# An encoder kernel: early small inputs, other banks for a second block, the router's comparisons first, a small expert last

## The chip, the cores and the metric

The kernel runs as one program on one core of a Trainium2 chip. The metric is device time in microseconds (us) for one execution, lower is better. Engines are TensorE (PE; PEld are its weight loads), VectorE (DVE), ScalarE (ACT), GpSimd (POOL) and SyncE (SP), which issues most of the transfers. Each runs its own list of instructions in order and waits for the others by semaphores.

## What is computed

A hybrid encoder of two layers on 256 tokens of width 1024, in float32. Cut to what matters here:

```python
def reference(x, positions, norm_mix, w_in_first, ..., norm_out):
    for l in range(DEPTH):                       # 2
        h = rmsnorm(x, norm_mix[l])
        proj = h @ (w_in_first if l == 0 else w_in_rest[l - 1])
        # columns of proj: RWKV-7 heads, differential attention, mean pooling
        x = x + jnp.concatenate([y_a, y_b, y_c], axis=-1) @ w_out[l]
        h = rmsnorm(x, norm_ffn[l])
        if l % 2 == 0:
            x = x + swiglu(h, ffn_gate[i], ffn_up[i], ffn_down[i])
        else:
            x = x + moe_swiglu(h, router[i], exp_gate[i], exp_up[i], exp_down[i])
    return rmsnorm(x, norm_out)

def moe_swiglu(h, router, w_gate, w_up, w_down):
    logits = t @ router
    top_val, top_idx = lax.top_k(logits, TOP_K)  # 2 of 8 experts
    gates = jax.nn.softmax(top_val, axis=-1)
    combine = jnp.sum(jax.nn.one_hot(top_idx, N_EXPERTS) * gates[..., None], axis=1)
    for e in range(N_EXPERTS):
        out = out + combine[:, e:e + 1] * swiglu(t, w_gate[e], w_up[e], w_down[e])
```

D_FF is 3584. Each expert has three matrices of 1024 x 3584.

## The kernel before, in words

Weights come in tiles of 128 x 1024 float32 (512 KB) through a ring of raw slots (`wload`). Most are split in two halves of a reduced format that TensorE takes in one pass: ACT casts the tile to the high half (L201, `whi`), VectorE subtracts that from the tile (L209, `wlo`; a few go to POOL), and the product is three matmuls (`mm3`): high x high, low x high, high x low. The loads are issued by SP in the order of their use (L198, L184); a load waits for its slot, a cast for its load and a free high slot.

**The start** (layer 0's mixer, 0 to some 195 us). `setup_x` loads the identity, the rows of small vectors and x on SP and transposes x on TensorE (L230). Then two weight loads follow, and six more in the k loop over the 1024 rows of `w_in_first`: eight steps of 8 blocks x 3 matmuls into four banks (L226). The constants (`consts`, `consts2`), `lambda_q`, `lambda_k` and `positions` are loaded on ACT's queue (L311, L313, L341, L353) behind ACT's work on the norm. VectorE's use of them (`rksel` L327, `lamq` L342, `posf` L355, `ang` L358) stands between its weight splits. After the k loop VectorE makes `u` from the sums (L551) and `us` from it (L548, L549), and goes on to the pooling sums `cs` and to splits of later weights.

**The dense layer** (some 195 to 435 us). 3584 columns go in seven blocks of 512. `gateup(c0)` makes gate and up sums of one block in four banks of the pool `pa`; VectorE scales them to `gu` (L1307). `down(c0 - 1)` runs after `gateup(c0)` and adds into four banks of `pr`. So each block's `gateup` takes the four `pa` banks again that the block before has used.

**The router** (some 616 us). TensorE makes the logits, VectorE copies them (`lg`, L1018), compares them pairwise (`cmp`, L1444 to L1447; the last of these multiplies by constants), sums the comparisons to ranks and makes the selection `sel` (L1449). TensorE counts it with a triangle of ones (`tri`), VectorE makes places `pos` (L1461) and the one-hot gather matrix `Pm` (L1555), and TensorE gathers the tokens of an expert. At the same time x is split in two halves, the high one on ACT (L1424), the low one on POOL (L1425, twice 128 x 1024), and the first expert weights are split; `EPOOL` names the tiles whose low half POOL makes. `keep_clock` issues matmuls whose result nobody reads.

**The experts** (some 616 to 1519 us). Experts 0 and 1 keep their places, the other six are put in places 2 to 7 by their counts of tokens, the three with the fewest in the places 2, 4 and 6. Those three are "few": at most 64 tokens, run with plain float32 weights, without splits. A step of a full expert is a block of 512 columns: 8 tiles for gate and up and 4 for down, 72 three-pass matmuls; seven steps are 84 tiles. A few expert has the same 84 tiles with fewer matmuls. `SEQ` is the order of the places. `down` of a step runs after the `gateup` of the next one; `silu` (L1651), `turn` and the sums of `combine` (L1743, L1754) or `combine_few` (L1685, L1694) are woven into the step behind. After the last step come the last `combine`, the norm and the output (`final`, L1841 to L1853). `issue_after` sets the place of an instruction in its own engine's list; it adds no wait between engines.

The order on VectorE, ACT, POOL and SP is set by a scheduler from these hints; TensorE's is the order in which the code is written.

Of the kernel before, what the change touches and what calls it, by code (L numbers as in the profile page):

```python
# [7 lines left out]
F32 = mybir.dt.float32  # L8
# [75 lines left out]
SEQ = (0, 2, 1, 3, 4, 5, 6, 7)  # L84
# [15 lines left out]
GC0 = 2  # L100
WARM = (7, 5)
# [5 lines left out]
class K:  # L107
# [172 lines left out]
    def setup_x(self, P):  # L280
# [18 lines left out]
    def setup(self, P):  # L299
        nc, A, cp, mc, v, dv = self.nc, self.A, self.cp, self.mc, self.v, self.dv  # L300
# [6 lines left out]
        self.rks, tmp = mc.tile([128, 4, 2], F32, name="rksel"), self.dtmp  # L307
# [3 lines left out]
        nc.scalar.dma_start(c, A["consts"][:, :C_W])  # L311
        self.c2 = cp.tile([128, C_ALL - C_IOTA], F32, name="consts2")
        nc.scalar.dma_start(self.c2, A["consts"][:, C_IOTA:])  # L313
# [20 lines left out]
    def setup2(self, sp):  # L334
        nc, A, cp, c = self.nc, self.A, self.mc, self.c
        q = nc.scalar

        lq = sp.tile([128, 256], F32, name="lamq", tag="s1k", bufs=2)
        lk = sp.tile([128, 256], F32, name="lamk", tag="s1k", bufs=2)
        for t_, nm in ((lq, "lambda_q"), (lk, "lambda_k")):  # L340
            q.dma_start(t_, bass.AP(tensor=A[nm].tensor, offset=A[nm].offset, ap=[[0, 128], [1, 256]]))  # L341
# [136 lines left out]
    def mixer(self, l, P):  # L478
# [801 lines left out]
    def ffn(self, l, P):  # L1280
# [9 lines left out]
        def gateup(c0):  # L1290
            bs = [self.bank() for _ in range(4)]
# [24 lines left out]
        def down(c0, ah, al, last=False):  # L1316
            if not acc:
                acc.extend(self.bank("pr") for _ in range(4))
# [8 lines left out]
            if not last:  # L1327
                for f in range(4):
                    w = ld(f)
                    for a in range(2):  # L1330
# [4 lines left out]
                          lambda a: self.norm_part((a,), (("pa",) * 4, ("pr", "pr", "pa", "pa"))[a]),  # L1335
# [12 lines left out]
    def moe(self, l, P):  # L1348
# [71 lines left out]

        x0 = [[P.tile([128, D], F32R, name=f"x{n}{a}", tag=("xp r0", "r1 r2")[a].split()[n]) for a in range(2)] for n in range(2)]
        for a in range(2):
            with self.tc.issue_after(self.hi) if a else nullcontext():
                nc.scalar.copy(x0[0][a], self.x[:, a])  # L1424
            nc.gpsimd.tensor_sub(x0[1][a], self.x[:, a], x0[0][a].bitcast(F32))  # L1425
        parts = [[[t_[:, k2 * 256:k2 * 256 + 256] for t_ in x0[n]] for n in range(2)] for k2 in range(4)]
        self.hi_after = self.hi
        ahead, self.ahead = self.ahead, []
        for n_ in range(len(ahead), XSPLIT + 3):
            self.early = [nc.gpsimd if n_ in EPOOL else nc.vector]  # L1430
            self.lo_after = self.pow if n_ > 3 else None
            ahead.append(wgu(0, 0, n_ // 2, n_ % 2))
            if n_ == 3:
                with self.tc.issue_after(self.w1):
                    for a in range(2):
                        self.stat(a, P.tile([128, D], F32, name="nsq", tag="gh0"))
# [481 lines left out]
```

## Time and profile before

| | us |
|---|---|
| median of three runs | 1536.27 (1534.88, 1536.27, 1536.39) |
| profiled execution | 1537.17 |
| its span, first to last instruction | 1535.4 |
| TensorE busy | 1454.0 (95%) |
| VectorE, ACT, POOL busy | 996.8, 812.5, 163.7 |
| HBM read | 431.75 MB, 282 GB/s over the span |
| mean granted clock | 0.982 |

Busy shares are means over stages with different limits. The chain is followed backwards from the last instruction to what released each step. In a timeline row the bracket holds the idle time of the engine just before and what ended it. "SPq" and "ACTq" are the issuing of transfers. [...]

### The profile page before, as it was taken

How to read it: one execution, taken by the hardware profiler on the slowest of the kernel's cores; microseconds unless marked ns; L12 is line 12 of the kernel's file. 1: busy time of each engine (PE TensorE's matmuls, PEld its weight loads, DVE VectorE, ACT ScalarE, POOL GpSimd, SP SyncE). 2: the span in 40 equal slices, each digit the busy share in tenths (PEclk: the TensorE clock that was granted, in tenths of full speed). 3: DMA queues.
4: the chain of work that ended last, by engine and by line, in shares of the span. 5: the costliest groups of instructions: out<-in, count | busy, mean ns of one | idle time of the engine just before them, and what ended most of it. 6: DMA issues, size and time to landing. Idle time of an engine off the chain costs nothing.

```text
span 1535.4 us, 27152 instructions
## 1 busy us (share of the span) xinstructions
PE 1454.0 (95%) x10215; PEld 1102.3 (72%) x10215; DVE 996.8 (65%) x1318; ACT 812.5 (53%) x1146; POOL 163.7 (11%) x153
## 2 busy tenths in 40 slices
PE   6889989999998999899998999999998999998996
PEld 6767789999987777688633688888534787435885
DVE  4875665556659755899511889898412897206896
ACT  4635454444445454688501778777302775205785
POOL 2442100000025323300000000011000000000001
PEclk9999999999999999999999999999999999999999
DMA  7322346666543238689799999999999999999991
GB/s 228 110 72 98 110 167 190 192 187 189 162 119 98 86 111 326 213 306 368 281 419 412 412 410 412 410 382 336 374 418 412 412 410 402 405 416 411 411 411 38
DMA packets 172457, 434.67 MB, mean 283 GB/s; under 512 B 14834, under 2 KB 18013, under 8 KB 172317
## 3 DMA queue, kind: packets, MB, share of 16 engines
q1 hardware_dynamic: 170924, 430.74, 75.5%
q8 instruction: 82, 1.34, 0.3%
q10 hardware_dynamic: 848, 0.99, 0.3%
q0 software_dynamic: 544, 1.12, 0.3%
q14 instruction: 59, 0.48, 0.1%
HBM read 431.75 MB, written 1.05 MB: 282 GB/s over the span
## 4 chain that ended last, share of the span: by engine, by line
PE 73%; DVE 10%; DMA 9%; ACT 4%; issue 3%; POOL 1%; ACTq 0%; SPq 0%; DVEq 0%; POOLq 0%
PE ps L226 71%; DMA r<-in_exp_up 5%; PE ps L230 3%; DMA r<-in_exp_gate 2%; DVE wlo L209 2%; DVE wlox L209 1%; DMA lamk<-in_lambda_k 1%; ACT whi L201 1%; DMA raw<-in_w_in_rest 1%; DVE us L549 0%; ACT whix L201 0%; DVE us L548 0%; ACT nsq L389 0%; DMA x<-in_x 0%; ACT hT_h L409 0%
## 5 line engine op out<-in xcount | busy, mean ns | idle before, releaser
L209 DVE TENSOR_TENSOR wlo<-r,whi 128x1024 fp32r<-128x1024 f32 x193 | 233.5, 1237 | 43.8 <-ACT whi L201 42.4
L201 ACT CAST whi<-r 128x1024 fp32r<-128x1024 f32 x196 | 202.7, 1055 | 37.2 <-DMA r<-in_exp_gate 17.4
L209 DVE TENSOR_TENSOR wlox<-r,whix 128x1024 fp32r<-128x1024 f32 x125 | 152.2, 1238 | 63.8 <-ACT whix L201 58.0
L201 ACT CAST whi<-raw 128x1024 fp32r<-128x1024 f32 x117 | 123.1, 1054 | 95.9 <-PE ps L226 86.0
L209 DVE TENSOR_TENSOR wlo<-raw,whi 128x1024 fp32r<-128x1024 f32 x106 | 133.9, 1267 | 55.0 <-ACT whi L201 54.5
L201 ACT CAST whix<-r 128x1024 fp32r<-128x1024 f32 x125 | 130.2, 1055 | 39.2 <-DMA r<-in_exp_gate 26.8
L226 PE MATMUL ps<-whi,gf 128*128 128x512 f32 x396 | 134.6, 398 | 0.0
L226 PE MATMUL ps<-r,gs 128*64 128x512 f32 (+1 forms) x636 | 131.1, 549 | 1.9 <-DMA r<-in_exp_up 1.9
L226 PE MATMUL ps<-fT,whi 128*128 128x256 f32 x544 | 99.3, 285 | 3.8 <-DVE gu L1307 3.4
L226 PE MATMUL ps<-whix,gf 128*128 128x512 f32 x276 | 95.4, 400 | 2.5 <-ACT whix L201 2.5
L226 PEld LDWEIGHTS ps<-r,gs 128*64 128x64 f32 x636 | 42.5, 136 | 72.6 <-issue 60.6
L1418 POOL TENSOR_TENSOR xp<-x,xp 128x512 fp32r<-128x512 f32 x12 | 22.6, 1886 | 628.9 <-ACT xp L1417 583.4
L226 PEld LDWEIGHTS ps<-fT,whi 128*128 128x128 f32 x544 | 85.0, 192 | 5.2 <-issue 4.0
L226 PEld LDWEIGHTS ps<-whi,gf 128*128 128x128 f32 x396 | 75.3, 190 | 18.6 <-issue 1.6
L1664 ACT COPY mah<-ps 128x512 f32<-128x512 f32 (+1 forms) x12 | 6.4, 532 | 142.2 <-PE ps L230 142.2
L226 PE MATMUL ps<-wlo,gf 128*128 128x512 f32 x198 | 78.5, 396 | 0.3
L226 PE MATMUL ps<-fT,wlo 128*128 128x256 f32 x272 | 77.2, 284 | 0.0
L209 DVE TENSOR_TENSOR wlox<-raw,whix 128x1024 fp32r<-128x1024 f32 x49 | 61.2, 1251 | 17.7 <-ACT whix L201 17.6
L226 PE MATMUL ps<-whi,mah 128*128 128x512 f32 x170 | 66.5, 391 | 0.0
L226 PE MATMUL ps<-wlo,mah 128*128 128x512 f32 x170 | 66.4, 390 | 0.0
L226 PE MATMUL ps<-whi,mal 128*128 128x512 f32 x170 | 66.2, 389 | 0.0
L226 PE MATMUL ps<-r,mah 128*64 128x512 f32 x264 | 63.8, 600 | 2.3 <-DMA r<-in_exp_down 1.8
(475 smaller groups left out, 3360.0 us busy)
## 6 DMA issues: line engine op xcount, KB each, us to landing
r<-in_exp_gate SPq DMA_DIRECT2D x184, 512.0 KB, 9.9
r<-in_exp_up SPq DMA_DIRECT2D x173, 512.0 KB, 9.9
r<-in_exp_down SPq DMA_DIRECT2D x171, 512.0 KB, 10.1
raw<-in_exp_down SPq DMA_DIRECT2D x48, 512.0 KB, 10.1
raw<-in_exp_up SPq DMA_DIRECT2D x43, 512.0 KB, 10.0
raw<-in_exp_gate SPq DMA_DIRECT2D x34, 512.0 KB, 9.9
raw<-in_w_in_first SPq DMA_DIRECT2D x22, 512.0 KB, 5.0
raw<-in_w_in_rest SPq DMA_DIRECT2D x22, 512.0 KB, 3.8
```

Of the source, the lines that this page charges most:

```text
L201: w1 = nc.scalar.copy(hi[:, :a * b], raw[:, :a * b])
L209: w2 = (early or nc.vector).tensor_sub(lo[:, :a * b], raw[:, :a * b], hi[:, :a * b].bitcast(F32))
L226: self.nc.tensor.matmul(out, lhsT, rhs, start=start, stop=stop, skip_group_check=skip_group_check)
L230: self.nc.tensor.transpose(out, in_, ident)
L1418: nc.gpsimd.tensor_sub(xl, xs, xh.bitcast(F32))
L1664: nc.scalar.copy(at, b)
```

## The change

Four things are put into one kernel.

1. The five small loads are issued by SP behind the first two weight loads (`setup_loads`). TensorE gets 7 matmuls without use ahead of the first transposition and 6 behind the norm (`keep_warm`). In each k step of the input projection, in both layers, the high half's 16 matmuls come first and the low half's 8 after them.
2. In the dense layer the first block's gate and up sums stay in `pa`, all others go to `pr`, and the down sums to `pa`; the banks of the norm behind it are exchanged to match.
3. In the router the comparisons, the selection and the places are written ahead of the split of x, whose low half goes from POOL to VectorE, behind `sel` and `pos`. `WARM[0]` goes from 7 matmuls to 4.
4. `SEQ` ends with places 7, 6 in place of 6, 7. The end of the program is made fit for a few expert: parts of the final norm are issued as soon as their quarter of y is summed.

```diff
-SEQ = (0, 2, 1, 3, 4, 5, 6, 7)
+SEQ = (0, 2, 1, 3, 4, 5, 7, 6)
...
-WARM = (7, 5)
+WARM = (4, 5)
...
+        self.idle = self.bank("py")
+        self.keep_warm(7)
         pb = self.bank("pr")
         self.tr(pb[:, :NROWS], rows, self.ident[:NROWS, :NROWS])
         nc.vector.tensor_copy(self.v, pb[:, :NROWS])
...
+    def keep_warm(self, n):
...
+        for _ in range(n):
+            self.mm(self.idle[:, :128], self.ident, self.ident, start=True, stop=True)
...
-        nc.scalar.dma_start(c, A["consts"][:, :C_W])
         self.c2 = cp.tile([128, C_ALL - C_IOTA], F32, name="consts2")
-        nc.scalar.dma_start(self.c2, A["consts"][:, C_IOTA:])
+        self.lq, self.lk = (sp.tile([128, 256], F32, name=n, tag="s1k", bufs=2) for n in ("lamq", "lamk"))
...
+    def setup_loads(self):
+        nc, A = self.nc, self.A
+        nc.sync.dma_start(self.c, A["consts"][:, :C_W])
+        for t_, nm in ((self.lq, "lambda_q"), (self.lk, "lambda_k")):
+            nc.sync.dma_start(t_, bass.AP(tensor=A[nm].tensor, offset=A[nm].offset, ap=[[0, 128], [1, 256]]))
+        nc.sync.dma_start(self.pi, A["positions"].rearrange("b (a p) -> p (b a)", p=128))
+        nc.sync.dma_start(self.c2, A["consts"][:, C_IOTA:])
+
+    def setup(self, P):
...
-        nc, A, cp, c = self.nc, self.A, self.mc, self.c
-        q = nc.scalar
...
-        lq = sp.tile([128, 256], F32, name="lamq", tag="s1k", bufs=2)
-        lk = sp.tile([128, 256], F32, name="lamk", tag="s1k", bufs=2)
-        for t_, nm in ((lq, "lambda_q"), (lk, "lambda_k")):
-            q.dma_start(t_, bass.AP(tensor=A[nm].tensor, offset=A[nm].offset, ap=[[0, 128], [1, 256]]))
+        nc, c, lq, lk = self.nc, self.c, self.lq, self.lk
...
-        pi = sp.tile([128, 2], I32, name="posi")
-        q.dma_start(pi, A["positions"].rearrange("b (a p) -> p (b a)", p=128))
...
-        nc.vector.tensor_copy(pf, pi)
+        nc.vector.tensor_copy(pf, self.pi)
...
+            self.setup_tiles(P)
...
                     ws.append(self.wload(A["w_in_first"].rearrange("(k p) c -> p k c", p=128)[:, q // 2:q // 2 + 1, 0:1024], 1, 1024))
+            self.setup_loads()
+            self.keep_warm(6)
...
         for k in range(KD):
             wh, wl = ws.pop(0) if ws else self.wload(wk[:, k:k + 1, 0:1024], 1, 1024)
-            for n_, f in enumerate(forder):
-                b = pa[n_ // 2][:, (n_ % 2) * 256:(n_ % 2) * 256 + 256]
-                self.mm3(b, hh[:, k], hl[:, k], wh[:, 0, f * 128:f * 128 + 128], wl[:, 0, f * 128:f * 128 + 128],
-                         k == 0 and n_ % 2 == 0, k == KD - 1, True)
...
+            for w, hs in ((wh, (hh, hl)), (wl, (hh,))):
+                for n_, f in enumerate(forder):
+                    b = pa[n_ // 2][:, (n_ % 2) * 256:(n_ % 2) * 256 + 256]
+                    for h in hs:
+                        self.mm(b, w[:, 0, f * 128:f * 128 + 128], h[:, k], start=k == 0 and n_ % 2 == 0 and w is wh and h is hh,
+                                stop=k == KD - 1 and w is wl, skip_group_check=True)
...
         def gateup(c0):
-            bs = [self.bank() for _ in range(4)]
...
+            bs = [self.bank("pr" if c0 else "pa") for _ in range(4)]
...
         def down(c0, ah, al, last=False):
             if not acc:
-                acc.extend(self.bank("pr") for _ in range(4))
+                acc.extend(self.bank("pa") for _ in range(4))
...
-                          lambda a: self.norm_part((a,), (("pa",) * 4, ("pr", "pr", "pa", "pa"))[a]),
+                          lambda a: self.norm_part((a,), (("pr",) * 4, ("pa", "pa", "pr", "pr"))[a]),
...
+        lj, le = (t_.to_broadcast([128, 2, NE, NE]) for t_ in (lg[:, :, None, :], lg[:, :, :, None]))
+        nc.vector.tensor_tensor(cmp[:, :, :, :NE], lj, le, op=ALU.is_gt)
+        nc.vector.tensor_tensor(cmp[:, :, :, NE:], lj, le, op=ALU.is_equal)
+        lt = c[:, C_LT - C_IOTA:C_LT - C_IOTA + 64].rearrange("p (e j) -> p e j", j=NE)
+        nc.vector.tensor_mul(cmp[:, :, :, NE:], cmp[:, :, :, NE:], lt[:, None].to_broadcast([128, 2, NE, NE]))
+        nc.vector.tensor_reduce(rank, cmp, axis=AX.X, op=ALU.add)
+        sel_ = nc.vector.tensor_scalar(sel, rank, 2.0, None, op0=ALU.is_lt).ins
+        ahead, self.ahead = self.ahead, []
+        idle, w0 = self.bank("py"), ahead[0][0]
+
...
+        keep_clock(WARM[0])
+        br = self.bank("px")
+        self.mm(br[:, 0:16], tri, sel.rearrange("p a e -> p (a e)"), start=True, stop=False, skip_group_check=True)
+        self.mm(br[:, 8:16], one, sel[:, 0], start=False, stop=True, skip_group_check=True)
+
+        pos_ = nc.vector.scalar_tensor_tensor(pos.rearrange("p a e -> p (a e)"), br[:, 0:16], 1.0, sel.rearrange("p a e -> p (a e)"),
+                                       op0=ALU.add, op1=ALU.mult).ins
...
         for a in range(2):
             with self.tc.issue_after(self.hi) if a else nullcontext():
                 nc.scalar.copy(x0[0][a], self.x[:, a])
-            nc.gpsimd.tensor_sub(x0[1][a], self.x[:, a], x0[0][a].bitcast(F32))
+            with self.tc.issue_after((sel_, pos_)[a]):
+                nc.vector.tensor_sub(x0[1][a], self.x[:, a], x0[0][a].bitcast(F32))
...
-        ahead, self.ahead = self.ahead, []
...
-            self.lo_after = self.pow if n_ > 3 else None
+            self.lo_after = self.pow if n_ > 3 else pos_
...
-        nc.vector.tensor_tensor(cmp[:, :, :, NE:], lj, le, op=ALU.is_equal)
-        lt = c[:, C_LT - C_IOTA:C_LT - C_IOTA + 64].rearrange("p (e j) -> p e j", j=NE)
-        nc.vector.tensor_mul(cmp[:, :, :, NE:], cmp[:, :, :, NE:], lt[:, None].to_broadcast([128, 2, NE, NE]))
-        nc.vector.tensor_reduce(rank, cmp, axis=AX.X, op=ALU.add)
-        nc.vector.tensor_scalar(sel, rank, 2.0, None, op0=ALU.is_lt)
...
-
-            for _ in range(n):
...
-        self.mm(br[:, 8:16], one, sel[:, 0], start=False, stop=True, skip_group_check=True)
-
-        nc.vector.scalar_tensor_tensor(pos.rearrange("p a e -> p (a e)"), br[:, 0:16], 1.0, sel.rearrange("p a e -> p (a e)"),
-                                       op0=ALU.add, op1=ALU.mult)
         keep_clock(WARM[1])
...
+                self.there = 0
...
+                    self.there = 2 * a + 2
...
+                        self.there = 2 * a + hf + 1
...
-                    st["s"] = silu(NE - 1, st["n"])
+                    st["s"] = silu(seq[-1][0], st["n"])
...
-                    st["o"] = turned(st["t2"])
+                    st["o"] = (turned_few if few(seq[-1][0]) else turned)(st["t2"])
...
-                if (e, c0) == (NE - 1, GC0):
+                if (e, c0) == (SEQ[-2], GC0):
...
-            for n_, _ in enumerate(side[-1]):
-                if n_ > 1:
+            done = 0
+            for _ in side[-1]:
+                while done < self.there:
                     next(out)
+                    done += 1
```

**SP at the start** (`raw` are weight loads).

Before:

```order
L294 DMA x<-in_x 128x1024 x2
L198 DMA raw_142<-in_w_in_first 128x1024
L198 DMA raw_156<-in_w_in_first 128x1024
L198 DMA raw_224<-in_w_in_first 128x1024
L198 DMA raw_254<-in_w_in_first 128x1024
L198 DMA raw_340<-in_w_in_first 128x1024
L198 DMA raw_375<-in_w_in_first 128x1024
L198 DMA raw_405<-in_w_in_first 128x1024
L198 DMA raw_435<-in_w_in_first 128x1024
```

With the change:

```order
L294 DMA x<-in_x 128x1024 x2
L198 DMA raw_164<-in_w_in_first 128x1024
L198 DMA raw_178<-in_w_in_first 128x1024
L325 DMA consts<-in_consts 128x1232
L327 DMA lamq<-in_lambda_q 128x256
L327 DMA lamk<-in_lambda_k 128x256
L328 DMA posi<-in_positions 128x2x1
L329 DMA consts_132<-in_consts 128x192
L198 DMA raw_257<-in_w_in_first 128x1024
L198 DMA raw_287<-in_w_in_first 128x1024
```

The five small loads stand between the second and the third weight load; `qks` (the tile 128x4x256) comes ahead of the `lora` loads further on.

**VectorE ahead of `u`** (`qTs`, `kTs`, `ARs`, `bkuvs`, `wlo` are splits of later weights).

Before:

```order
L209 TENSOR_TENSOR qTs<-raw_470,qks 128x1024
L209 TENSOR_TENSOR kTs<-raw_575,kTs 128x1024
L209 TENSOR_TENSOR ARs<-raw_608,ARs 128x1024
L372 TENSOR_TENSOR ang<-ang 128x16
L209 TENSOR_TENSOR bkuvs<-raw_644,bkuvs 128x1024
L373 TENSOR_SCALAR cos<-ang 128x16
L551 TENSOR_TENSOR u<-ps_172,R 128x512
L551 TENSOR_TENSOR u<-ps_173,R 128x512
L551 TENSOR_TENSOR u<-ps_174,R 128x512
L551 TENSOR_TENSOR u<-ps_175,R 128x512
```

With the change:

```order
L209 TENSOR_TENSOR wlo_421<-raw_419,whi_420 128x1024
L209 TENSOR_TENSOR qTs<-raw_484,qks 128x1024
L209 TENSOR_TENSOR wlo_451<-raw_449,whi_450 128x1024
L209 TENSOR_TENSOR kTs<-raw_589,kTs 128x1024
L209 TENSOR_TENSOR ARs<-raw_622,ARs 128x1024
L209 TENSOR_TENSOR bkuvs<-raw_658,bkuvs 128x1024
L209 TENSOR_TENSOR wlo_695<-raw_693,whi_694 128x1024
L209 TENSOR_TENSOR wlo_759<-raw_757,whi_758 128x1024
L569 TENSOR_TENSOR u<-ps_205,R 128x512
L569 TENSOR_TENSOR u<-ps_206,R 128x512
```

`wlo_695` and `wlo_759` are the splits that stood at `wlo_681` and `wlo_745`, after `us` and the sums `cs`; they now stand ahead of `u`, and the last `ang` and `cos` ahead of all of these.

**The router, on POOL and on VectorE** (L209 are low halves of expert weights).

POOL before:

```order
L1393 TENSOR_SCALAR tri<-consts_295,vecs 128x128
L1425 TENSOR_TENSOR x_7157<-x,x_7155 128x1024
L1425 TENSOR_TENSOR x_7158<-x,x_7156 128x1024
L209 TENSOR_TENSOR wlo_7147<-r_7128,whi_7145 128x1024
L209 TENSOR_TENSOR wlo_7148<-r_7129,whi_7146 128x1024
```

POOL with the change:

```order
L1412 TENSOR_SCALAR tri<-consts_132,vecs 128x128
L209 TENSOR_TENSOR wlo_7161<-r_7142,whi_7159 128x1024
L209 TENSOR_TENSOR wlo_7162<-r_7143,whi_7160 128x1024
L391 TENSOR_TENSOR nr<-nr,dvecs 128x1 x2
L209 TENSOR_TENSOR wlo_7212<-r_7145,whi_7211 128x1024
```

VectorE before:

```order
L1018 COPY lg<-ps_7088 128x16
L1444 TENSOR_TENSOR cmp<-lg 128x16x8
L1445 TENSOR_TENSOR cmp<-lg 128x16x8
L1447 TENSOR_TENSOR cmp<-cmp,consts_295 128x16x8
L1448 TENSOR_REDUCE rank<-cmp 128x16
L1449 TENSOR_SCALAR sel<-rank 128x16
L1461 SCALAR_TENSOR_TENSOR pos<-ps_7201,sel 128x16
L1555 TENSOR_TENSOR Pm<-consts_295,pos 128x512
L209 TENSOR_TENSOR wlo_7170<-r_7130,whi_7169 128x1024
```

VectorE with the change:

```order
L1036 COPY lg<-ps_7102 128x16
L1443 TENSOR_TENSOR cmp<-lg 128x16x8
L1444 TENSOR_TENSOR cmp<-lg 128x16x8
L1446 TENSOR_TENSOR cmp<-cmp,consts_132 128x16x8
L1447 TENSOR_REDUCE rank<-cmp 128x16
L1448 TENSOR_SCALAR sel<-rank 128x16
L1469 TENSOR_TENSOR x_7186<-x,x_7184 128x1024
L1461 SCALAR_TENSOR_TENSOR pos<-ps_7180,sel 128x16
L1469 TENSOR_TENSOR x_7187<-x,x_7185 128x1024
L1575 TENSOR_TENSOR Pm<-consts_132,pos 128x512
L209 TENSOR_TENSOR wlo_7199<-r_7144,whi_7198 128x1024
```

The two subtractions of x go from POOL, where the weight halves follow `tri` directly now, to VectorE, one on each side of `pos`.

## Rows read from the trace of the kernel before

**Rows 1.** The page, part 4: the chain that ended last, by engine.

```profile
PE 73%; DVE 10%; DMA 9%; ACT 4%; issue 3%; POOL 1%; ACTq 0%; SPq 0%; DVEq 0%; POOLq 0%
```

**Rows 2.** The chain in time, 0 to 60 us: start, us, what.

```profile
18.45 12.19 DMA lamk<-in_lambda_k
```

**Rows 3.** Timeline of VectorE, 15 to 62 us: start, us, instruction, idle before.

```profile
44.08 2.48 DVE L551 TENSOR_TENSOR u<-ps,R 128x512 f32<-128x512 f32 x4
...
56.36 1.19 DVE L209 TENSOR_TENSOR wlo<-raw,whi 128x1024 fp32r<-128x1024 f32 x1
```

**Rows 4.** Timeline and stretches of TensorE, 25 to 47 us; clock after the count.

```profile
26.41 0.38 PE L226 MATMUL ps<-hT_h,wlo 128*128 128x256 f32 x1 [0.89 <-DVE wlo L209]
...
32.53 0.39 PE L226 MATMUL ps<-hT_h,wlo 128*128 128x256 f32 x1 [2.67 <-DVE wlo L209]
...
46.10 0.36 PE L226 MATMUL ps<-hT_h,qks 128*128 128x256 f32 x1 [3.74 <-DVE u L551]
...
27.00:30.00 3.00, 2.86 (x26) 1.00 0.94 254
33.00:36.00 3.00, 3.00 (x16) 0.50 0.68 182
```

**Rows 5.** DMA issues and rates, 0 to 60 us: KB each, us to landing.

```profile
GB/s 0 69 273 404 426 418 423 153 11 109 240 175 231 208 337 309 325 319 215 293 176 8 65 300 246 199 325 295 324 302 158 238 1 16 0 0 0 0 0 191
...
consts<-in_consts ACTq DMA_DIRECT2D x1, 616.0 KB, 7.5
...
lamk<-in_lambda_k ACTq DMA_DIRECT2D x1, 128.0 KB, 12.2
```

**Rows 6.** Dense layer: groups of the page, TensorE's timeline, stretches 220 to 230.

```profile
L201 ACT CAST whi<-raw 128x1024 fp32r<-128x1024 f32 x117 | 123.1, 1054 | 95.9 <-PE ps L226 86.0
...
L226 PE MATMUL ps<-fT,whi 128*128 128x256 f32 x544 | 99.3, 285 | 3.8 <-DVE gu L1307 3.4
...
221.60 0.77 PE L226 MATMUL ps<-fT,whi 128*128 128x256 f32 x2 [2.96 <-DVE gu L1307]
...
220.00:225.00 5.00, 3.12 (x13) 2.88 (x14) 4.15 (x10) 2.64 (x8) 0.00 (x0) 0.55 0.35 105
225.00:230.00 5.00, 5.00 (x36) 5.00 (x36) 1.23 (x1) 1.47 (x2) 0.00 (x0) 0.77 0.04 6
```

**Rows 7.** Timeline of all engines at the router, 616 to 633 us.

```profile
617.41 0.28 DVE L1445 TENSOR_TENSOR cmp<-lg 128x128 f32<-128x128 f32 x1
617.57 4.73 POOL L1425 TENSOR_TENSOR x<-x,x 128x1024 fp32r<-128x1024 f32 x2
617.72 2.37 DVE L1447 TENSOR_TENSOR cmp<-cmp,consts 128x128 f32<-128x128 f32 x1
...
620.58 1.75 DVE L1449 TENSOR_SCALAR sel<-rank 128x16 f32<-128x16 f32 x1
...
622.26 5.14 POOL L209 TENSOR_TENSOR wlo<-r,whi 128x1024 fp32r<-128x1024 f32 x2
...
622.48 0.37 PE L226 MATMUL ps<-sel,tri 128*128 128x16 f32 x2 [3.89 <-DVE sel L1449]
...
625.09 3.39 DVE L209 TENSOR_TENSOR wlo<-r,whi 128x1024 fp32r<-128x1024 f32 x1
```

**Rows 8.** Experts: ACT's timeline, the chain at the end, GB/s of 40 slices.

```profile
855.78 0.69 ACT L1651 ACTIVATE msilu<-ps,rs 128x512 f32<-128x512 f32 x1
...
1172.69 1.04 ACT L201 CAST whix<-r 128x1024 fp32r<-128x1024 f32 x1 [11.26 <-DMA r<-in_exp_gate]
...
1192.03 0.69 ACT L1651 ACTIVATE msilu<-ps,rs 128x512 f32<-128x512 f32 x1
...
1419.75 16.38 PE ps L226 x72
...
1510.48 9.07 PE ps L226 x38
...
GB/s 228 110 72 98 110 167 190 192 187 189 162 119 98 86 111 326 213 306 368 281 419 412 412 410 412 410 382 336 374 418 412 412 410 402 405 416 411 411 411 38
```

More of the change, by code (lines that the diff above doesn't have):

```diff
@@ L297, in setup_x, with setup_tiles @@
         nc.vector.tensor_copy(self.v, pb[:, :NROWS])
-    def setup(self, P):
-        nc, A, cp, mc, v, dv = self.nc, self.A, self.cp, self.mc, self.v, self.dv
+    def keep_warm(self, n):
+        for _ in range(n):
+            self.mm(self.idle[:, :128], self.ident, self.ident, start=True, stop=True)
+    def setup_tiles(self, sp):
+        cp, mc = self.cp, self.mc
         self.Z = mc.tile([128, 3, 2, 2, 128], F32, name="Z")
@@ L306, in setup @@
         c = self.c = mc.tile([128, C_W], F32, name="consts")
-        self.rks, tmp = mc.tile([128, 4, 2], F32, name="rksel"), self.dtmp
+        self.rks = mc.tile([128, 4, 2], F32, name="rksel")
         self.nlam = mc.tile([128, 2], F32, name="nlam")
@@ L310, in setup @@
         mc.tile([128, 16], F32, name="mcpad")
-        nc.scalar.dma_start(c, A["consts"][:, :C_W])
         self.c2 = cp.tile([128, C_ALL - C_IOTA], F32, name="consts2")
-        nc.scalar.dma_start(self.c2, A["consts"][:, C_IOTA:])
+        self.lq, self.lk = (sp.tile([128, 256], F32, name=n, tag="s1k", bufs=2) for n in ("lamq", "lamk"))
+        self.pi = sp.tile([128, 2], I32, name="posi")
+    def setup_loads(self):
[6 more added lines that the diff above has]
+    def setup(self, P):
+        nc, v, dv, c, tmp = self.nc, self.v, self.dv, self.c, self.dtmp
         sh = v[:, ROW_SHIFT:ROW_SHIFT + 32].rearrange("p (l i k) -> p l i k", l=2, i=2)
@@ L1419, in part_x @@
             return [xh[:, a] for a in range(2)], [xl[:, a] for a in range(2)]
[L1421 to L1424, printed above, removed]
-            nc.gpsimd.tensor_sub(x0[1][a], self.x[:, a], x0[0][a].bitcast(F32))
-        parts = [[[t_[:, k2 * 256:k2 * 256 + 256] for t_ in x0[n]] for n in range(2)] for k2 in range(4)]
-        self.hi_after = self.hi
-        ahead, self.ahead = self.ahead, []
-        for n_ in range(len(ahead), XSPLIT + 3):
-            self.early = [nc.gpsimd if n_ in EPOOL else nc.vector]
-            self.lo_after = self.pow if n_ > 3 else None
[L1432 to L1436, printed above, removed]
-        first_run[0] = True
-        self.hi_after = self.lo_after = None
         bc = lambda t_: t_[:, :, None].to_broadcast([128, 2, NE])
@@ L1459, in moe @@
         self.mm(br[:, 8:16], one, sel[:, 0], start=False, stop=True, skip_group_check=True)
-        nc.vector.scalar_tensor_tensor(pos.rearrange("p a e -> p (a e)"), br[:, 0:16], 1.0, sel.rearrange("p a e -> p (a e)"),
-                                       op0=ALU.add, op1=ALU.mult)
+        pos_ = nc.vector.scalar_tensor_tensor(pos.rearrange("p a e -> p (a e)"), br[:, 0:16], 1.0, sel.rearrange("p a e -> p (a e)"),
+                                       op0=ALU.add, op1=ALU.mult).ins
+        x0 = [[P.tile([128, D], F32R, name=f"x{n}{a}", tag=("xp r0", "r1 r2")[a].split()[n]) for a in range(2)] for n in range(2)]
+        for a in range(2):
+            with self.tc.issue_after(self.hi) if a else nullcontext():
+                nc.scalar.copy(x0[0][a], self.x[:, a])
+            with self.tc.issue_after((sel_, pos_)[a]):
+                nc.vector.tensor_sub(x0[1][a], self.x[:, a], x0[0][a].bitcast(F32))
+        parts = [[[t_[:, k2 * 256:k2 * 256 + 256] for t_ in x0[n]] for n in range(2)] for k2 in range(4)]
+        self.hi_after = self.hi
+        for n_ in range(len(ahead), XSPLIT + 3):
+            self.early = [nc.gpsimd if n_ in EPOOL else nc.vector]
+            self.lo_after = self.pow if n_ > 3 else pos_
+            ahead.append(wgu(0, 0, n_ // 2, n_ % 2))
+            if n_ == 3:
+                with self.tc.issue_after(self.w1):
+                    for a in range(2):
+                        self.stat(a, P.tile([128, D], F32, name="nsq", tag="gh0"))
+        first_run[0] = True
+        self.hi_after = self.lo_after = None
         keep_clock(WARM[1])
@@ L1737, in combine @@
             def combine(e, acc):
+                self.there = 0
                 yh = P.tile([128, D], F32R, name="myh", tag="myh")
```

## The prediction

> **What bounds the kernel now.** I read the views in this order: the page's busy shares and chain, the chain of waits at the start, the timelines of the three places where the change acts, and the stretches of the experts. Of the chain that ends last 73% is matmul time, 10% VectorE, 9% DMA [rows 1]. So there is no single stall to remove. What can be had are the holes between matmuls, and one change of pace in the last three experts. The profiled execution took 1537.17 us, 0.9 us above the median of the three runs (1536.27 us). I sum against the execution and apply the sum to the median. About 0.2% (3.1 us) is what a measurement of this kernel can tell from no change.
>
> **A, the early small inputs.** The chain of the start runs 12.19 us along one transfer, lambda_k, which ACT's queue issues only at 18.45 us [rows 2]. VectorE runs in order, so its weight halves stand behind the instructions that want these inputs, and TensorE waits for them twice, 0.89 and 2.67 us [rows 4]. [...] Together 0.89 + 2.67 + 1.6 = 5.2 us.
>
> The change moves the five loads onto SP's queue, behind x and two weight loads and ahead of the six other weights. SP now issues five more instructions there, and every later load of the queue stands behind 616 + 128 + 128 + 1 + 96 = 969 KB. From 4.5 to 10.5 us the transfers move 404 to 426 GB/s (slices of 1.5 us) [rows 5], so that is 969 KB / 418 GB/s = 2.4 us of delay for weights 3 to 8. x and four weights (3 MB) are across by about 12 us, so the inputs land at about 12 to 13 us and weight 3 at about 14.5 us. A k step has 24 matmuls of 0.11 us, 2.7 us; the first starts at 11.9 us, so the third is wanted at about 17.3 us. The delay is hidden by some 3 us. If that cover were gone, each us of lateness would be one us of the start.
>
> The 13 added warming matmuls (7 and 6) lie ahead of x and behind the norm, where TensorE waits anyway; if they ran into the block they would cost at most 13 x 0.2 = 2.6 us, and they may give back up to 1.7 us, as the block's first 18 matmuls run at the lower clock. I take 0 for both. Taking the two high passes ahead of the low pass gives VectorE 16 matmuls, 1.8 us, more per step; it is the reason why I count the whole of the two waits.
>
> VectorE is the next limit: u starts at 44.08 us, after the split before it, and TensorE's next work, 46.10 us, waited 3.74 us for u [rows 3, 4]. In the new order two more splits stand ahead of u, and two fewer behind it. They are 1.2 us each [rows 3], so 2.4 us moves from behind u to ahead of it, partly into VectorE's idle time. I count 1.3 us of that as gained. **A = -5.2 - 1.3 = -6.5 us.** Bounds: -4 if the splits ahead of u hold it, -9 if the warm start and all of the 2.4 us come on top (5.2 + 2.4 + 1.7 = 9.3). Layer 1's input projection gets the same order of passes; no wait for a low half stands there, so 0.
>
> [...]
>
> **B, the dense layer's second block.** The group row of the dense gate and up matmuls has 3.4 us of idle time that ended with VectorE's gu: the second block wants the four banks that the first has just left, and gu still reads them [rows 6]. The longest piece is 2.96 us. It is followed by a stretch at the lower clock: 0.55 on average in 220 to 225 us, 0.77 in 225 to 230 us. With 3.12 and 5.00 us of busy TensorE that is 3.12 x 0.5 + 5.00 x 0.23 = 2.7 us of lost pace. In the other banks nothing has to be left, and the weights lie ready: where ACT's casts of such weights wait, it is for TensorE [rows 6]. The down sums now go to the first block's banks, but a whole gate and up block lies between, so gu is long done. **B = -3.4 - 2.7 = -6 us**; -3.4 if the clock falls all the same.
>
> **C, comparisons first.** Today the comparisons' multiplication takes 2.37 us where its neighbour of the same shape takes 0.28, and the selection 1.75 us: each ends with one of the two POOL subtractions that form x's low half (4.73 us for two). TensorE waits 3.89 us for the selection [rows 7]. The diff takes these two subtractions from POOL and puts them on VectorE behind the selection. But the rows of POOL show that the next thing in its order is a weight half of the same shape and also of two operands, and that it waits for nothing later. It starts in the same place. What such a POOL instruction does to VectorE is seen further on: VectorE's own split takes 3.39 us while POOL runs two of them, 5.14 us [rows 7]. So I expect the comparisons to be held just as long, to about 622.4 us. Then VectorE has 2 x 1.2 us more to do before the gather matrix, and gains about as much, since POOL is done by then (the split behind the matrix 3.39 to 1.2 us). **C = 0**, bounds -4 (the 3.89 us go) and +1.5 (most of the two subtractions, 2.4 us, on the path).
>
> A reader of the diff alone would book the -4. [...]
>
> **D, the small expert last.** A full expert has 84 tiles of 512 KB; a step of 12 tiles is 16.38 us and a transposition of some 0.4 us [rows 8], 1.40 us a tile, TensorE's pace. A small one (at most 64 tokens) needs less TensorE time and goes at the transfers' pace, 512 KB at the page's 412 GB/s = 1.27 us a tile. Before, the small one stands between two full ones, and the transfers end long before TensorE: the last of the page's 40 slices, 38.4 us, has 38 GB/s where those ahead have 411 [rows 8]. Put last, the small one follows the transfers closely. But a second full expert behind a full one holds the transfers back (336 and 374 GB/s where that happens today, slices 28 and 29), so they will end later than now. The trace has the new sequence, full, full, small, once: from the first silu of the first (855.78 us) to 1172.69 us, when three tiles of the small one are still to land: 316.9 + 3 x 1.27 = 320.7 us, and 0.9 us for the last tile's matmuls. The end of today, from the same mark (1192.03) to the last matmul (1510.48 + 9.07 = 1519.55), is 327.5 us [rows 8]. The difference is -5.9 us. The end behind it (an evacuation, a transposition, half as many sums) is shorter by some 0.5 us in instructions, but less of it can be taken ahead; I give it +1. **D = -5 us**, bounds -8 and -2.
>
> Sum: -6.5 - 6 + 0 - 5 = -17.5 us. What is gained ahead of the experts is kept, as their transfers wait for free slots, and so for TensorE, over long stretches.
>
> **Rivals.**
> 1. *One gain is not there* (0.20). The start is held by the splits or by late weights, or the transfers end as late as before. Speaks for it: most slices of the experts stand at 402 to 419 GB/s as it is, so little is left to move earlier. A or D at 0 gives 1524 to 1525 us, both 1530.
> 2. *The comparisons come free* (0.13): VectorE gets ahead of POOL's weight half, the 3.89 us go. 1536.3 - 17.5 - 4 = 1515 us. Against it: POOL is ready as early as it was.
> 3. *Slower* (0.03): the five loads on one queue are served one at a time. With the times from issue to landing, 7.5 us for the constants and 12.2 us for each lambda [rows 5], weight 3 would land at 10.5 + 7.5 + 2 x 12.2 = 42.4 us, 25 us after it is wanted: -17.5 + 25 = +7.6, 1544 us. It decides from 35 us on (17.3 + 17.5). Against it: the rate row shows x and the weights following one another on one queue without a gap.
> 4. *The change doesn't do what it says* (0.02): the places are filled by other waits, within 0.2%, 1534 to 1539 us.
>
> **Numbers.** The forecast has 0.62: 1536.3 - 17.5 = 1519 us. The lower end takes A and D at their far bounds and B as it is (-9 - 6 - 8 = -23), with a little of rival 2: 1511. The upper end takes in one gain lost and B at -3.4: 1528. Faster by over 0.2%: 0.62 + 0.20 + 0.13 = 0.95; within: 0.02; slower: 0.03.
>
> **What would show it.** A: constants landing before 15 us, no wait for a low half in the first block, u before 39 us. B: no wait for gu and the full clock from 217 to 230 us. C: the multiplication and the selection still over 1.5 us, ending with POOL's weight halves. D: no full step after the last transfer, and the last three experts in some 322 us. If u starts later than 42 us, or the last transfer's end stays as far from the last matmul as it is, the sum is wrong there.

## The result, and the profile after

The changed kernel takes 0.9936 of the time before (95% interval 0.992 to 0.9953), which is -9.8 us (-12.3 to -7.2): 1528.24 us median of eight runs against 1536.33. The forecast was -17.5 us. The profiled execution took 1525.09 us with a span of 1523.2 us, so it is one of the faster ones; the eight runs lie between 1524.12 and 1531.07 us. That spread is itself a finding, see the last section.

**Start.** SyncE's timeline, then the transfers' table (KB each, us to landing), VectorE's and TensorE's timelines of the changed kernel:

```profile
3.62 0.44 SPq L325 DMA_DIRECT2D consts<-in_consts  x1
4.10 0.44 SPq L327 DMA_DIRECT2D lamq<-in_lambda_q  x1
4.59 0.45 SPq L327 DMA_DIRECT2D lamk<-in_lambda_k  x1
...
consts<-in_consts SPq DMA_DIRECT2D x1, 616.0 KB, 8.7
lamq<-in_lambda_q SPq DMA_DIRECT2D x1, 128.0 KB, 8.5
lamk<-in_lambda_k SPq DMA_DIRECT2D x1, 128.0 KB, 8.9
```

```profile
16.07 0.42 DVE L356 TENSOR_TENSOR lamq<-lamq,lamk 128x256 f32<-128x256 f32 x1
...
31.37 1.23 DVE L209 TENSOR_TENSOR qTs<-raw,qks 128x1024 fp32r<-128x1024 f32 x1 [4.25 <-ACT qks L201]
...
37.29 1.23 DVE L209 TENSOR_TENSOR bkuvs<-raw,bkuvs 128x1024 fp32r<-128x1024 f32 x1 [1.14 <-ACT bkuvs L201]
39.57 2.51 DVE L209 TENSOR_TENSOR wlo<-raw,whi 128x1024 fp32r<-128x1024 f32 x2 [1.06 <-ACT whi L201]
42.00 1.28 DVE L569 TENSOR_TENSOR u<-ps,R 128x512 f32<-128x512 f32 x2
```

```profile
34.95 1.10 PE L226 MATMUL ps<-hT_h,wlo 128*128 128x256 f32 x8
44.40 0.58 PE L226 MATMUL ps<-hT_h,qks 128*128 128x256 f32 x1 [8.34 <-DVE u L569]
```

The constants land at 3.62 + 8.7 = 12.3 us, lambda_k at 4.59 + 8.9 = 13.5 us, as forecast, and neither wait for a low half is left ([rows 4] had 0.89 and 2.67 us). TensorE is through with its block at about 36 us. But u starts only 2.1 us earlier than before (42.00 against 44.08 [rows 3]), behind the two splits of 39.57 us, and TensorE stands 8.34 us where it stood 3.74.

**Dense layer.** The group row, TensorE's first matmul of the layer, and the two stretches of 5 us where the first block ends (each engine's busy time, the clock, DMA share, GB/s):

```profile
L226 PE MATMUL ps<-fT,whi 128*128 128x256 f32 x544 | 98.2, 284 | 2.7 <-DVE fT L424 2.7
...
189.84 0.47 PE L226 MATMUL ps<-fT,whi 128*128 128x256 f32 x2 [2.69 <-DVE fT L424]
...
212.00:217.00 5.00, 5.00 (x44) 5.00 (x44) 3.65 (x4) 3.20 (x5) 0.00 (x0) 1.00 0.64 206
217.00:222.00 5.00, 5.00 (x45) 5.00 (x44) 4.92 (x10) 4.34 (x10) 0.00 (x0) 1.00 0.40 107
```

The wait for gu is gone and TensorE runs through at a clock of 1.00; [rows 6] had 3.12 us busy at 0.55. But a wait that the kernel before doesn't have now stands at the layer's start: 2.69 us for `fT`, the layer's input, whose low half VectorE makes. It isn't there with the banks alone (e2), and comes with the first part of the change; see "The start taken apart".

**Router.** Timeline of all engines:

```profile
612.35 0.28 DVE L1444 TENSOR_TENSOR cmp<-lg 128x128 f32<-128x128 f32 x1
612.52 4.70 POOL L209 TENSOR_TENSOR wlo<-r,whi 128x1024 fp32r<-128x1024 f32 x2
612.67 2.35 DVE L1446 TENSOR_TENSOR cmp<-cmp,consts 128x128 f32<-128x128 f32 x1
...
615.05 0.42 DVE L1447 TENSOR_REDUCE rank<-cmp 128x16 f32<-128x256 f32 x1
...
615.50 1.75 DVE L1448 TENSOR_SCALAR sel<-rank 128x16 f32<-128x16 f32 x1
...
617.40 0.58 PE L226 MATMUL ps<-sel,tri 128*128 128x16 f32 x2 [4.55 <-DVE sel L1448]
```

Of the lines that [rows 7] shows, only POOL's has changed: it now works on weight halves. 2.35 and 1.75 us are what they were with x's subtractions (2.37 and 1.75), and TensorE waits 4.55 us.

**The last experts.** The first silu, the chain at the end, the sums' copy, and the page's rates:

```profile
1184.19 0.70 ACT L1671 ACTIVATE msilu<-ps,rs 128x512 f32<-128x512 f32 x1
...
1496.35 9.81 DMA r<-in_exp_down
1506.16 0.04 issue
1506.20 1.10 PE ps L226 x4
1507.33 0.59 ACT mys L1706
...
GB/s 266 80 78 99 100 206 188 189 193 182 138 188 44 73 112 329 217 311 364 284 419 413 412 410 412 410 389 345 373 419 412 410 411 410 360 353 373 384 417 244
```

From the first silu to the last matmul 1506.20 + 1.10 - 1184.19 = 323.1 us, where the forecast had 321.6 and before had 327.5 [rows 8]. The chain ends with a transfer, and one tile's matmuls follow it. It lands 322.0 us after the first silu (1496.35 + 9.81 - 1184.19), where the forecast had 320.7. The second full expert holds the transfers back as expected (360, 353, 373 GB/s).

### The profile page after: what moved, and what is told of

It reads as the page before. It is cut to its first block, busy times and chain, and to the rows that moved or that the text cites. A ratio compares the mean times of both kernels' runs of the same rounds, so it can differ in the third digit from the quotient of the medians.

```text
span 1523.2 us, 27196 instructions
## 1 busy us (share of the span) xinstructions
PE 1450.9 (95%) x10238; PEld 1106.2 (73%) x10238; DVE 993.1 (65%) x1320; ACT 813.3 (53%) x1146; POOL 158.9 (10%) x151
## 4 chain that ended last, share of the span: by engine, by line
PE 75%; DMA 11%; DVE 7%; ACT 3%; issue 2%; POOL 1%; SPq 0%; POOLq 0%; ACTq 0%; DVEq 0%
PE ps L226 73%; DMA r<-in_exp_down 3%; DMA r<-in_exp_up 3%; PE ps L230 3%; DMA r<-in_exp_gate 2%; DMA raw<-in_w_in_first 1%; DVE wlo L209 1%; DVE wlox L209 1%; DMA raw<-in_w_in_rest 1%; DMA raw<-in_exp_up 1%; ACT whi L201 1%; DMA x<-in_x 0%; DVE BK L682 0%; ACT pr L1221 0%; POOL rn L639 0%
## 5 line engine op out<-in xcount | busy, mean ns | idle before, releaser
L209 DVE TENSOR_TENSOR wlo<-r,whi 128x1024 fp32r<-128x1024 f32 x193 | 232.5, 1232 | 37.7 <-ACT whi L201 36.4
L209 DVE TENSOR_TENSOR wlox<-r,whix 128x1024 fp32r<-128x1024 f32 x124 | 150.3, 1233 | 37.6 <-ACT whix L201 36.3
L209 DVE TENSOR_TENSOR wlo<-raw,whi 128x1024 fp32r<-128x1024 f32 x106 | 131.5, 1245 | 48.3 <-ACT whi L201 47.8
L201 ACT CAST whix<-r 128x1024 fp32r<-128x1024 f32 x124 | 129.1, 1057 | 28.8 <-DMA r<-in_exp_gate 15.9
L1437 POOL TENSOR_TENSOR xp<-x,xp 128x512 fp32r<-128x512 f32 x12 | 26.0, 2170 | 624.1 <-ACT xp L1436 624.1
L209 DVE TENSOR_TENSOR wlox<-raw,whix 128x1024 fp32r<-128x1024 f32 x50 | 62.4, 1252 | 19.9 <-ACT whix L201 19.9
L1672 DVE SCALAR_TENSOR_TENSOR msilu<-ps,rs,msilu 128x512 f32<-128x512 f32 (+1 forms) x47 | 34.2, 729 | 47.8 <-PE ps L226 31.3
L201 ACT CAST whix<-raw 128x1024 fp32r<-128x1024 f32 x50 | 52.6, 1053 | 23.9 <-PE ps L226 23.1
```

The source lines that it names most:

```text
L201: w1 = nc.scalar.copy(hi[:, :a * b], raw[:, :a * b])
L209: w2 = (early or nc.vector).tensor_sub(lo[:, :a * b], raw[:, :a * b], hi[:, :a * b].bitcast(F32))
L1437: nc.gpsimd.tensor_sub(xl, xs, xh.bitcast(F32))
L1672: nc.vector.scalar_tensor_tensor(sl, bs[1], rs, sl, op0=ALU.mult, op1=ALU.mult)
```

## The experiments

All with the kernel before as the comparison on the same chip. "Clock" is the mean granted clock, averaged over the runs of a kernel; before it was 0.9802 to 0.9807.

| run | ratio (95% interval) | us of 1535 | clock |
|---|---|---|---|
| e1 start alone | 1.0008 (0.9991 to 1.0025) | +1.2 | 0.977 |
| e2 banks alone | 0.9969 (0.9957 to 0.9981) | -4.8 | 0.984 |
| e3 router alone | 1.001 (1.0 to 1.0019) | +1.5 | 0.980 |
| e4 small expert last alone | 0.9983 (0.9973 to 0.9994) | -2.6 | 0.981 |
| e5 start, splits behind u | 1.0007 (0.9991 to 1.0024) | +1.1 | 0.978 |
| e6 start, hole filled | 1.0043 (1.0026 to 1.0059) | +6.6 | 0.979 |
| e7 router, POOL held | 0.9982 (0.9966 to 0.9998) | -2.8 | 0.982 |
| e8 all but the start | 0.9937 (0.9912 to 0.9961) | -9.7 | 0.983 |
| e9 e8 with POOL held | 0.9915 (0.9897 to 0.9933) | -13.0 | 0.984 |
| e10 e9 and the early loads | 0.9896 (0.9875 to 0.9917) | -16.0 | 0.982 |
| e11 early loads alone | 0.9973 (0.9963 to 0.9984) | -4.1 | 0.981 |
| e12 order of passes alone | 1.0023 (1.0007 to 1.004) | +3.5 | 0.977 |

**The four parts alone.** e1 takes the hunks of the start and of the input projections, e2 those of the banks, e3 those of the router with `WARM`, e4 `SEQ` and the end of the program. One line of each:

```diff
+            self.setup_loads()
+            bs = [self.bank("pr" if c0 else "pa") for _ in range(4)]
+                nc.vector.tensor_sub(x0[1][a], self.x[:, a], x0[0][a].bitcast(F32))
+SEQ = (0, 2, 1, 3, 4, 5, 7, 6)
```

> Only the start: early small inputs, warming matmuls, high passes first in both layers. The forecast's term, -6.5 us: about 1530. Split theory (the two splits that now stand ahead of u take back most of it): u at 42.0 us as in the changed kernel, -2 at u, and -2 to -3 in all: about 1533.5. Clock theory (the rest goes where the granted clock now falls in other places): layer 0's mixer ends 5 us earlier as in the changed kernel, and layer 1's mixer takes 3 to 4 us longer than before.

> Only the banks of the dense layer. The forecast's term, -6 us: no wait for gu, no lower clock behind it, about 1530. Rival, clock theory: the 6 us are there at the end of the dense layer, but layer 1's mixer, which starts 6 us earlier, gets the lower clock in other stretches and gives back up to 4 of them: 1530 to 1534, with more spread between runs.

> Only the router's comparisons first and x's low half on VectorE. The forecast's term, 0: the multiplication takes over 2 us and the selection over 1.5 us, since POOL's weight half starts in the same place; 1536 within 1 us. Rival: they take 0.3 us and TensorE's wait of 3.9 us goes: 1532.

> Only the small expert last. The forecast's term, -5 us: about 1531, the last three experts in 322 to 323 us from the first silu of the first to the last matmul. Rival: the transfers end so much later that nothing is left, 1536. Nothing ahead of the experts differs, so the spread between runs should be that of the kernel before, 2 to 3 us; if it is 7 us, the spread comes from the end.

Two terms stand near the forecast: banks -4.8 (-6.6 to -2.9, forecast -6) and router +1.5 (0.0 to +2.9, forecast 0). The small expert has half of its -5: -2.6 (-4.1 to -0.9); its runs spread over 5.8 us, and so do those of the kernel before on that chip. The start isn't there: +1.2 us, where -6.5 was forecast. Its twelve runs lie between 1527.58 and 1545.79 us, and they follow the clock: 0.984 in the fastest, 0.971 in the slowest, a correlation of -0.96. In the profiled one the mean clock is 0.67 in the stretch in which u is made, two thirds of it at 0.50, and 0.52 where the dense layer starts:

```profile
36.00:51.50 15.50, 5.59 (x29) 5.40 (x29) 12.31 (x21) 8.02 (x13) 3.73 (x3) 0.67 0.67 226
195.00:202.00 7.00, 5.82 (x28) 5.85 (x29) 6.24 (x12) 5.67 (x9) 0.55 (x1) 0.52 0.33 98
```

Read along a straight line through its runs, the start alone takes 1532.0 us at a clock of 0.981 and the kernel before 1535.2. By that line some 3 us of gain are there, and the clock takes more than that. A line through runs is an argument and no experiment. What e1's clock theory expected of the two mixers didn't come in this execution: the dense layer's first matmul starts 3.9 us later than before (196.18 against 192.33), not 5 us earlier, and layer 1's mixer takes less than 1 us longer, not 3 to 4.

**Two repairs of the start.**

```diff
# e5, in wload
+        if self.behind_u and self.wn in (5, 6):
+            after = self.behind_u
# e6, behind the input projection of layer 0
+            self.keep_warm(36)
```

> Only the start, as in the first of the runs, with the two weight splits put back behind u. Split theory: u at 38.5 us instead of 42.0, TensorE's hole ahead of it some 5 us instead of 8.3, and the whole at -3 to -5 us: 1530 to 1532. Clock theory alone (what counts is how long TensorE stands idle, and where): a mean granted clock back near 0.980 is what brings the time down, about 1532. If neither holds, 1535 to 1537 as with the start alone.

> Only the start, with 36 matmuls whose result nobody reads (some 7.7 us) put between the input projection's last matmul and the next use of TensorE. They shorten no wait. Clock theory: no stretch at the lower clock between 36 and 50 us, mean clock 0.980 or more, less spread, about 1532. If the clock has no part in it: the time of the start alone, 1537.

With the splits behind it u starts at 39.45 us, 4.6 us before its old time, and TensorE's hole is 5.08 us, as expected. But nothing of it is left in the whole: +1.1 us (-1.4 to +3.7), where -3 to -5 was expected. VectorE then waits for ACT's part of `us`, and the mean clock is about as low as in e1 (0.978). Even in the profiled execution, the fastest of its eleven (1530.34 us), the lead is gone at the end of the mixer: the dense layer's first matmul starts at 194.04 us (before 192.33). The split theory fell:

```profile
39.45 2.47 DVE L571 TENSOR_TENSOR u<-ps,R 128x512 f32<-128x512 f32 x4
44.45 0.88 DVE L568 SCALAR_TENSOR_TENSOR us<-u,vecs,us 128x255 f32<-128x255 f32 x2 [2.53 <-ACT us L565]
```

e6 tells little. The hole is filled (0.25 us left), and behind it, from 44.72 to 47.10 us, 21 matmuls follow one another at 0.11 us, the pace that [rows 4] has at a clock of 1.00 (2.86 us for 26), as the clock theory had it. But the added matmuls also made the scheduler put another instruction ahead of `cs` on ACT, and TensorE waits for that. The mean clock is 0.979 (e1: 0.977), not 0.980 or more, and the time is over both figures that were expected. Whether filling the hole alone would help stays open:

```profile
44.38 0.39 PE L226 MATMUL ps<-hT_h,qks 128*128 128x256 f32 x1 [0.25 <-DVE u L571]
...
53.84 1.99 PE L226 MATMUL ps<-us,lora 128*128 128x256 f32 x4 [3.87 <-ACT cs L620]
```

**The router with POOL held.** A POOL copy of one column of x's second low half stands ahead of POOL's weight halves; the rest is e3.

```diff
+        pw = nc.gpsimd.tensor_copy(P.tile([128, 1], F32, name="pw"), x0[1][1][:, 0:1].bitcast(F32)).ins
-            self.lo_after = self.pow if n_ > 3 else pos_
+            self.lo_after = self.pow if n_ > 3 else pw if n_ in EPOOL else pos_
```

> Only the router's part, and POOL's weight halves wait for the second subtraction of x (one POOL copy of a column ahead of them). [...] Rival: the weight halves come so late that the first expert waits for them and 0 to 1 us is left: 1535.

```profile
619.36 0.29 DVE L1427 TENSOR_TENSOR cmp<-cmp,consts 128x128 f32<-128x128 f32 x1
...
620.14 0.17 DVE L1429 TENSOR_SCALAR sel<-rank 128x16 f32<-128x16 f32 x1
...
620.46 0.37 PE L226 MATMUL ps<-sel,tri 128*128 128x16 f32 x2 [0.93 <-DVE sel L1429]
...
623.28 5.72 POOL L209 TENSOR_TENSOR wlo<-r,whi 128x1024 fp32r<-128x1024 f32 x2
```

Nothing was changed on VectorE, and the same two instructions take 0.29 and 0.17 us instead of 2.35 and 1.75. So POOL's instruction in that place is the cause of their length. The forecast for this run was 0.3 and 0.2 us, and 1532 us in all; 0.9982 of 1535.3 is 1532.5 us. The freed place is worth 4.3 us against e3, and the two intervals (0.0 to +2.9 and -5.2 to -0.3) lie apart.

**All but the start, and the best version.** e8 leaves out the hunks of e1; e9 adds e7's lines; e10 adds `setup_tiles` and `setup_loads` without the warming matmuls and with the passes in the old order.

> All of the change but the start: banks, router, small expert last. Sum of the parts alone, -4.8 + 1.5 - 2.7 = -6 us: 1529. If it is as fast as the whole change (0.9936 of before, 1525.5) the start gives nothing in company either; if it is 3 us slower, the start gives 3 us there.

> Banks, small expert last and the router's part with POOL's weight halves held behind x's second subtraction; the start as in the kernel before. The run without the start (0.9937) and the 2.5 us that freeing the comparisons gave between router and experts: 1523 to 1524, about 0.992, which would beat both kernels. Rival: the expert's transfers set the pace behind the router, nothing is left of the 2.5 us, 0.9937.

> The same and the five early loads, without the warming matmuls and without high passes first. Theory of the lost start (u comes only 2 to 4 us earlier, and a lower mean clock takes that back): same time as without the loads, within 1.5 us, mean clock lower by 0.002 or more. Rival: it was the warming matmuls or the order of the passes that cost the clock: 3 us faster than without the loads, 1520.

e8 is as fast as the whole change: the start gives nothing in company either. But e8 missed the sum of its parts: -9.7 us (-13.5 to -6.0), where -6 was expected. e9 came out as expected, 0.9915; against e8 that is some 3 us, and the two intervals overlap. In e10 the time came as the rival had it: with the loads alone out of the start's parts it is 0.9896, -16.0 us, and 1519.57 us median, the fastest of all. Against e9 that is 3 us, and these two intervals overlap as well. The clock came as the first theory had it, 0.002 lower than in e9.

**The start taken apart.** e11 is before with the five early loads; e12 is before with this hunk alone:

```diff
+            for w, hs in ((wh, (hh, hl)), (wl, (hh,))):
+                for n_, f in enumerate(forder):
```

> Of the change only the five early loads, alone. Theory of the lost start: within 1.5 us of before, mean clock 0.978. Rival as in the run with all but them: 1532 and a clock of 0.980 or more.

> Of the change only the order of the passes in the two input projections (the low half's 8 matmuls behind the high half's 16). The first wait for a low half, 0.89 us, goes, the second (for lambda_k) stays: 0 to -1 us at the start, nothing in layer 1, mean clock as before, 1535. If the clock is 0.978 and the time 1536 or more, this order is what costs the clock.

The two have opposite signs: the loads -4.1 us (-5.7 to -2.5), as the rival of e11 had it, the order of the passes +3.5 us (+1.1 to +6.1). With the loads alone the waits of 0.89 and 2.67 us are gone but for 0.51 us, so hardly anything was left for the order to take:

```profile
34.95 0.38 PE L226 MATMUL ps<-hT_h,wlo 128*128 128x256 f32 x1 [0.51 <-DVE wlo L209]
```

In e12 the wait of 0.89 us is gone, but TensorE is only sooner at its hole, and u comes 1.6 us later than before. That has a cause in VectorE's list: with the new order the scheduler put one weight split, which waits 1.26 us for ACT's cast, ahead of u, where the kernel before has none. Stretches with a mean clock of 0.59 and 0.51 follow:

```profile
44.49 1.23 DVE L209 TENSOR_TENSOR wlo<-raw,whi 128x1024 fp32r<-128x1024 f32 x1 [1.26 <-ACT whi L201]
...
45.71 2.48 DVE L554 TENSOR_TENSOR u<-ps,R 128x512 f32<-128x512 f32 x4
...
47.74 0.55 PE L226 MATMUL ps<-hT_h,qks 128*128 128x256 f32 x1 [8.64 <-DVE u L554]
...
39.00:51.40 12.40, 3.76 (x18) 3.69 (x18) 9.44 (x17) 10.65 (x18) 3.33 (x3) 0.59 0.67 226
82.00:96.00 14.00, 14.00 (x140) 12.95 (x128) 8.55 (x20) 3.40 (x7) 5.53 (x6) 0.51 0.14 39
```

All five kernels with the new order (the changed kernel with 0.978, e1, e5, e6, e12) have mean clocks of 0.977 to 0.979, all nine without it, before and both with the early loads among them, 0.980 to 0.984. Four of the five also have the warming matmuls; only e12 has the order by itself. Along straight lines through the runs on the same chip, e12 takes 1535.7 us at a clock of 0.981 and before 1535.6, so by these lines the order costs little beside the clock. But 0.981 is the highest clock of e12's runs, and the later u is no matter of the clock.

The warming matmuls were not tried alone. All four kernels with them (the changed kernel, e1, e5, e6) wait 2.68 to 2.70 us for `fT` ahead of the dense layer's first matmul, e12 waits 0.63 us there, and the other nine go on without a wait at that matmul. In e1 the whole start is 1.8 us slower than the loads and the order add up to (-4.1 + 3.5), within the intervals. Whether the wait comes from the matmuls, from the bank that they take ahead of all others, or only in company with the loads and the order, is not shown.

## Why the prediction was right or wrong

**The direction and the range held; the size didn't: -9.8 us for -17.5. A failed, and D came at half.** 0.9936 of 1536.3 is 1526.4 us, inside 1511 to 1528, whose upper end allowed for one gain lost. The sum was -6.5 - 6 + 0 - 5 = -17.5. Measured alone: +1.2, -4.8, +1.5, -2.6, together -4.7; the whole is -9.8. Each of the four has an interval of about 2 us on either side and the whole one of 2.5, so the difference between -4.7 and -9.8 is at the edge of what these runs can tell. e8 shows as much without the start, -9.7 for -5.9, so the difference need not lie there. Whether the parts help one another stays open. With -4.7 the time would have been 1531.6 us, outside the range; as far as the prediction goes, that the range held is in part luck.

- *A, the waits.* The landing times were right (12.3 and 13.5 us), and so was the cover: the weights behind the five loads came in time. No run shows the 1.6 us that the sum takes for the lower clock behind the second wait: by [rows 4] 16 matmuls take 3.00 us at a clock of 0.50 and 26 take 2.86 us at 1.00, so the 16 lose some 1.2 us; in the changed kernel the clock is 1.00 from 24 to 36 us. The five loads alone gave -4.1 us, the lower bound of the gain ("-4 if the splits ahead of u hold it"). The step that failed is "Taking the two high passes ahead of the low pass gives VectorE 16 matmuls, 1.8 us, more per step". I took it as the reason to count both waits in full, and booked no cost. The loads take both waits away without it, but for 0.51 us, and alone it costs 3.5 us: u comes later, and the mean clock is lower (0.977 against 0.980). How much of the cost is the clock's is argued from the lines, not shown. The same step's 0 for layer 1 rested only on the absence of a wait, and looked at no clock.
- *A, the warming matmuls.* I took 0 for them. In the changed kernel the block's matmuls follow one another at 0.12 us from the start, where before about 13 of them (I had 18) came at 0.21 us, near the 0.19 us (3.00 / 16) that [rows 4] has at a clock of 0.50, although the clock column reads 1.00 for that stretch (11.9 to 15.6 us). Against that stands the wait of 2.7 us for `fT`, which I didn't look for.
- *A, u.* I named VectorE as the next limit and still counted 1.3 us for two splits moved ahead of it. They hold u by about 2.5 us (42.00 against 39.45 in e5), and "u before 39 us" was missed; but e5, without them, was no faster as a whole.
- *B* came as forecast: no wait, a clock of 1.00 (212 to 222 us), and behind the second block the work of the profiled execution stands some 6 us further ahead than in front of it. -4.8 us (-6.6 to -2.9) by the runs.
- *C* held. With x's subtractions in POOL's place the multiplication takes 2.37 us and the selection 1.75 us [rows 7], with weight halves there 2.35 and 1.75, and with the place empty 0.29 and 0.17 (e7). The rank's reduction, which stands between the two, took 0.42 us in all three. Why the two are held and the reduction isn't, no run shows. The rival's condition, POOL's weight half out of the way, was then made in e7, and its 4 us came (4.3).
- *D* was right in kind and too large: 323.1 us for the last three experts in place of 321.6, 324.2 in e4's own trace, and the end behind it no shorter than before, 1523.2 - 1507.3 = 15.9 us. That makes 3.3 to 4.4 us; -2.6 (-4.1 to -0.9) was measured. The transfers ended later than in the pattern of the earlier experts that I copied.

The rival that fits is the first, one gain that is not there. Its mechanism as I wrote it was late weights or the splits. The splits do hold u in the trace, but e5 without them gave nothing back. The gain of the loads was there, and what stood beside it in the same part, the order of the passes above all, took it back.

## What to carry to other kernels

Where four things go into one kernel, time each alone: here a loss of 3.5 us hid in the same part as a gain of 4.1, and a version without it and without the warming matmuls, with POOL held, is 6 us faster than the change. An edit that let TensorE run ahead of the engine that feeds its next stage didn't shorten the chain here; it gathered the idle time in one place (8.64 us in e12, 3.74 before), and the mean clock of that stretch was 0.59, so read the clock column before such an edit is costed at nothing. An instruction moved off an engine leaves its place to the next in that engine's list (here two weight halves, 4.70 us, where x's 4.73 us had stood), so look at the order of the engine that was relieved. And where a scheduler sets the order, an edit on one engine can move instructions on the others, so read their order again behind every edit.

## What the runs showed of the hardware that was not expected

Much of the spread of one kernel's times goes with the clock, in some kernels more than in others: the correlation is -0.96 in e1 and -0.62 to -0.74 in the kernel before, but -0.41 in the changed kernel and -0.22 in e6. Twelve runs of the start alone, on one chip, span 18 us; 0.001 of mean granted clock goes with 1.3 us there, with 0.6 to 0.75 us in the kernel before. About half of the time at the lower clock (0.50), or more, lies in the mixers (in the profiled executions 27 of 55 us before, 39 of 63 us in the changed kernel), where TensorE stands idle for 41 of 373 us before, and in the dense layer for 5 of 243 us. Where that time lies differs from kernel to kernel: layer 1's mixer, from its first matmul to the ranks, takes 185.4 us in the changed kernel's profiled execution and 180.4 us in that of the kernel before, although in the mixer itself nothing was changed but the order of passes:

```profile
494.00:508.00 14.00, 13.22 (x179) 12.46 (x180) 8.23 (x17) 3.40 (x7) 5.10 (x5) 0.52 0.14 40
```

The same 14 us of the kernel before, which is some 10 us further back in its work there, have a mean clock of 0.77. But e11, with the old order, has lost as much at this place in its profiled execution (185.3 us), so a single profile can't say what an edit does to the clock; the means over runs can. Why the mean is lower with the new order of passes (0.977 in e12) was not tried apart and stays open. The profiles point to layer 0: for the same 1980 or so matmuls between u and the dense layer TensorE is busy for 137.6 to 139.9 us in e1, e5, e6 and e12, and for 133.6 to 137.4 us in the nine kernels with the old order; the changed kernel, with 134.3 us, doesn't fit, and each is one execution.
